# Winograd products that accumulate onto one another in PSUM, in the MLP of a two-layer hybrid encoder

## Chip, cores and metric

One core of a Trainium2 chip runs the whole kernel. The metric is the device time of one execution in microseconds (us). Before the change the median of three runs is 3536.11 us (3528.11 to 3537.86).

## The reference

The trunk has two layers over 1024 tokens of width 1024, in float32. Layer 0 mixes by grouped-query attention, layer 1 by a bidirectional gated DeltaNet. Each mixer is followed by the same MLP, and this MLP is what the change touches:

```python
def conv_ffn(h, w_up, conv_w, conv_b, w_down):
    u = depthwise_conv_centred(h @ w_up, conv_w, conv_b)
    a, b = jnp.split(u, 2, axis=-1)
    return (jax.nn.silu(a) * b) @ w_down
...
        h = h + conv_ffn(rmsnorm(h, norm_ffn[i]), ffn_w_up[i], ffn_conv_w[i],
                         ffn_conv_b[i], ffn_w_down[i])
```

D_FF is 2816, so `w_up` is 1024 x 5632 and `w_down` 2816 x 1024. The convolution runs over three neighbouring tokens.

## The kernel before, in words

Activations lie transposed: features on the 128 partitions, the 1024 tokens along the free axis in two halves of 512 (`HALVES`). A float32 product is made of three TensorE products: both operands are split into a high part (a rounding cast on ScalarE, L109) and a low part (a subtraction on VectorE or GpSimd, L110), and high x high, high x low and low x high are added in PSUM. `dense` (L126) issues them, 128x128 weights against 512 columns, one PSUM bank of 128x512 as target.

Both projections use Winograd's form of Strassen's scheme: the operands are cut in 2 x 2 blocks, seven block products are made of sums of blocks, and the four output blocks are sums of the products.

**Up projection** (`UpProjection.run`, L975). A loop over 22 values of `f`. Each makes seven products of 12 matmuls; in the order of the code before they are p1, p2 ("11", "21"), p5 ("t1"), p6 ("t2"), p7 ("t3"), p4 ("t4") and p3 ("22"). `operands` (L948) loads four 128x512 blocks of weights and forms four sums `s` of them, two on POOL and two on DVE. `product` (L967) splits an operand and calls `dense`. Seven additions on DVE (`add`, L981) and one ScalarE copy (L991) build `ua` and `ub` (128x1024) from the PSUM banks. Then the convolution: one ScalarE Identity (L1010) and two VectorE scalar_tensor_tensor (L1011, L1013) for each of `ua` and `ub`, a Silu (L1016), a product (L1017). `DownProjection.take` (L1035) stores the result in DRAM, and for odd `f` forms on POOL the token sums that the down projection will need (L1039).

**Down projection** (`DownProjection.run`, L1076). Seven products, "11", "21", "t1", "t2", "t3", "t4", "22", one after the other. Each has 11 rounds `p` (`NP`), and in a round four output tiles `m` of three matmuls each: 12 matmuls a round, 132 a product, into four banks. Weights come by DMA (`load`, L1071), tokens by DMA from DRAM and a split (`tokens`, L1064; `gh`, `gl`). `w5` (L1134) adds the blocks `a21` and `a22` into `s`; `w6` (L1144) subtracts `a11` from it; t3 takes a21 - a11, formed on POOL, and 22 takes a12 - s, formed on POOL (L1163). The residual comes back from DRAM through `res`, three buffers (L1101).

The banks matter here. PSUM has eight. The pool `mm` has two tiles of two banks (`big()`), the ring `sp` has four single banks (`bank()`). A product of the down projection before takes one `mm` tile and two `sp` banks:

```python
            acc = t.big()
            accs = [acc[:, HALVES[0]], acc[:, HALVES[1]], t.bank(), t.bank()][:len(ms)]
```

so two consecutive products stand in different banks.

The order on each engine is set by a scheduler that takes instructions by priority as they become ready; `ahead` raises the priority of a block. It is fixed when the kernel is built, and each engine then runs its list in that order, waiting at the head for what is not ready.

Of the kernel before, what the change touches and what calls it, by code (L numbers as in the profile page):

```python
# [9 lines left out]
F32 = mybir.dt.float32  # L10
# [3 lines left out]
ALU = mybir.AluOpType  # L14
# [4 lines left out]
P = 128  # L19
S = 1024  # L20
# [6 lines left out]
NP = NFF // 2  # L27
# [14 lines left out]
class Trunk:  # L42
# [80 lines left out]
            out += [(hi[:, i * n:(i + 1) * n], lo[:, i * n:(i + 1) * n]) for i in range(c)]  # L123
        return out

    def dense(self, acc, w, ys, halves=HALVES, first=True, last=True):  # L126

        n = len(ys)
        one = len(halves) == 1
        for k, ((hi, lo), (yh, yl)) in enumerate(zip(w, ys)):  # L130
            for t, (a, y) in enumerate(((hi, yh), (hi, yl), (lo, yh))):
                for hs in halves:
                    self.nc.tensor.matmul(acc if one else acc[:, hs], lhsT=a, rhs=y[:, hs],  # L133
                                          start=(first and k + t == 0), stop=(last and k == n - 1 and t == 2))

    def half_dense(self, acc, w, ys, i):

# [730 lines left out]


class UpProjection:  # L870
# [64 lines left out]
                put("22", k, xs, y[k + 4][1])  # L935

    def start(self, n):
        for _ in range(n):
            p1, p25, ua = self.begin()
            for k, (acc, name) in enumerate(((p1, "11"), (p25[:, HALVES[0]], "21"))):  # L940
                self.t.dense(acc, self.t.weights(self.src(len(self.started), 0, k)), self.b[name], [slice(0, H2)])
            self.nc.scalar.copy(out=ua[:, HALVES[0]], in_=p1)
            self.started.append((p25, ua))

    def begin(self):
        return self.t.bank(), self.t.big(), self.us.tile([P, S], F32, name="ua", bufs=2)

    def operands(self, f):  # L948
        nc, raw = self.nc, []
# [14 lines left out]
        return {"p1": (a11, "11"), "p2": (a12, "21"), "p5": (s[0], "t1"), "p6": (s[1], "t2"), "p7": (s[2], "t3"),  # L964
                "p4": (a22, "t4"), "p3": (s[3], "22")}

    def product(self, acc, ops, name):  # L967
        x, col = ops[name]
        hi, lo = self.t.pair(self.t.wp, "w", H2)
        self.t.split(x, hi, lo, self.nc.gpsimd if name in ("p6", "p4") else self.nc.vector)  # L970
        w = [(hi[:, k * P:(k + 1) * P], lo[:, k * P:(k + 1) * P]) for k in range(4)]
        self.t.dense(acc, w, self.b[col], [slice(0, H2)])
        return acc

    def run(self, up, down):  # L975

        t, nc = self.t, self.nc
        self.up, cw = up, self.cw

        def add(out, x, acc):  # L980
            nc.vector.tensor_tensor(out=out, in0=acc, in1=x, op=ALU.add)  # L981

        for f in range(NFF):
            early = f < len(self.started)
            with t.ahead(early):
                ops = self.operands(f)
            if early:
                p25, ua = self.started[f]
            else:
                p1, p25, ua = self.begin()  # L990
                nc.scalar.copy(out=ua[:, HALVES[0]], in_=self.product(p1, ops, "p1"))  # L991
                self.product(p25[:, HALVES[0]], ops, "p2")
            p2, p5 = (p25[:, hs] for hs in HALVES)
            ub = up.tile([P, S], F32, name="ub", bufs=2)
            u2 = self.us.tile([P, H2], F32, name="u2", bufs=1)
            (ua0, ua1), (ub0, ub1) = ([u[:, hs] for hs in HALVES] for u in (ua, ub))
            with t.ahead(early):
                self.product(p5, ops, "p5")
                p6 = self.product(t.bank(), ops, "p6")
            add(u2, ua0, p6)  # L1000
            add(ua0, ua0, p2)
            add(ua1, u2, p5)
            add(ub1, u2, self.product(t.bank(), ops, "p7"))
            add(ub0, ub1, self.product(t.bank(), ops, "p4"))
            add(ub1, ub1, p5)
            add(ua1, ua1, self.product(t.bank(), ops, "p3"))
            ts = []
            for u, i, n in ((ua, f, 2), (ub, NFF + f, 1)):
# [12 lines left out]


class DownProjection:
# [52 lines left out]
    def run(self):  # L1076
# [9 lines left out]
            t.split(x, *pair)  # L1086
            return pair

        def product(name, x, ms=range(4), ys=None):

            acc = t.big()
            accs = [acc[:, HALVES[0]], acc[:, HALVES[1]], t.bank(), t.bank()][:len(ms)]
            for p in range(NP):
                w = x(p)
                y = ys(p) if ys else self.tokens(name, p)
                for acc, m in zip(accs, ms):
                    t.dense(acc, [[a[:, m * P:(m + 1) * P] for a in w]], [y], [slice(0, H2)],
                            first=p == 0, last=p == NP - 1)
            return list(zip(ms, accs))

        def residual(m, i):  # L1101
            r = gm.tile([P, H2], F32, name="res", bufs=3)
# [16 lines left out]
            return weights(self.load(x, 0, 0, p), pairs[p - 3] if p > 2 else None)  # L1119

        a11 = []
        acc = product("11", w1, ys=lambda p: self.ready[p] if p < G_FIRST else self.tokens("11", p))
        base = [x[:, hs] for x in [t.base(i, F32) for i in range(8)] for hs in HALVES]
        u, a12 = base[:4], base[4:4 + NP]
        for m, acc in acc:
            nc.scalar.copy(out=u[m], in_=acc)
            add(h(m, 0), acc, residual(m, 0))
        w2 = lambda p: weights(self.load(a12[p], 0, 1, p), [one(n, p, F32R) for n in ("a21", "a22")])
        for m, acc in product("21", w2):
            add(h(m, 0), acc, h(m, 0))  # L1130
            done(m, 0, m == 0)
        a21, a22, s = (slot(n) for n in ("a21", "a22", "s"))

        def w5(p):  # L1134
            for j, a in enumerate((a21, a22)):
                self.load(a[p], 1, j, p)
            add(s[p], a21[p], a22[p])
            return weights(s[p])

        for m, acc in product("t1", w5):  # L1140
            for k in (m, 4 + m):
                add(h(k, 1), acc, residual(k, 1))

        def w6(p):  # L1144
            if p < A_LATE:
# [1 line left out]
            sub(s[p], s[p], a11[p])  # L1147
            return weights(s[p])

        for m, acc in product("t2", w6):  # L1150
            add(u[m], acc, u[m])
            add(h(m, 1), h(m, 1), u[m], nc.gpsimd)
        for m, acc in product("t3", lambda p: weights(sub(a21[p], a11[p], a21[p], nc.gpsimd))):
            add(u[m], acc, u[m])
            add(h(4 + m, 1), h(4 + m, 1), u[m], nc.gpsimd)
            done(4 + m, 1, m == 0)
            r = residual(4 + m, 0)
            add(h(4 + m, 0), r, u[m], nc.gpsimd)
        for m, acc in product("t4", lambda p: weights(a22[p])):
            add(h(4 + m, 0), acc, h(4 + m, 0))  # L1160
            done(4 + m, 0, False)
        for p in range(NP):
            sub(a12[p], a12[p], s[p], nc.gpsimd)  # L1163
        sides = [list(zip(*(slot(n, F32R) for n in names))) for names in (("a21", "a11"), ("a22", "s"))]
        for p in range(NP):
            weights(a12[p], sides[0][p])
            self.tokens("22", p, sides[1][p])
        for ms in ((0, 1, 2), (3,)):
            for m, acc in product("22", lambda p: sides[0][p], ms, lambda p: sides[1][p]):
                add(h(m, 1), acc, h(m, 1))  # L1170
                done(m, 1, False)

# [200 lines left out]
```

## Time and profile before

| | |
|---|---|
| median of 3 runs | 3536.11 us (3528.11 to 3537.86) |
| the profiled execution, its own time | 3534.62 us |
| its span, first to last instruction | 3532.7 us |
| mean granted TensorE clock | 0.98 |
| busy share PE / DVE / ACT / POOL | 94 / 75 / 47 / 31 % |
| up projection, layer 0 / layer 1 | about 670 to 1099 / 2850 to 3297 us |
| down projection, layer 0 / layer 1 | about 1099 to 1350 / 3297 to 3518 us |

Read it from the engine that is nearly always busy. PE is busy for 94% of the span, so time can be gained or lost where PE stands idle or runs at the lower clock. Everything that the other engines do beside a busy PE costs nothing. A wait is printed behind an instruction as [idle before <-releaser]. In the trace's names `mm` and `sp` are PSUM tiles, `wh`/`wl` and `gh`/`gl` split weights and tokens; in the down projection `a`, `s` and `base` are blocks of weights.

### The profile page before, as it was taken

How to read it: one execution, taken by the hardware profiler on the slowest of the kernel's cores; microseconds unless marked ns; L12 is line 12 of the kernel's file. 1: busy time of each engine (PE TensorE's matmuls, PEld its weight loads, DVE VectorE, ACT ScalarE, POOL GpSimd, SP SyncE). 2: the span in 40 equal slices, each digit the busy share in tenths (PEclk: the TensorE clock that was granted, in tenths of full speed). 3: DMA queues.
4: the chain of work that ended last, by engine and by line, in shares of the span. 5: the costliest groups of instructions: out<-in, count | busy, mean ns of one | idle time of the engine just before them, and what ended most of it. 6: DMA issues, size and time to landing. Idle time of an engine off the chain costs nothing. (4 is left out here: it accounts for less than half of the span.)

```text
span 3532.7 us, 54926 instructions
## 1 busy us (share of the span) xinstructions
PE 3309.3 (94%) x20042; PEld 2655.5 (75%) x20042; DVE 2631.9 (75%) x4273; ACT 1648.1 (47%) x2918; POOL 1097.3 (31%) x1190
## 2 busy tenths in 40 slices
PE   7999999899999898999999999999898989999988
PEld 6877878677878686777777777777676867777776
DVE  5325886899997876767767777776763889999685
ACT  4224664433434353555555455555542544434442
POOL 1111230445452423132223333222320254454141
PEclk9999999999999999999999999999999999999999
DMA  3331016323324641333242433324355723232733
GB/s 123 103 103 63 31 34 203 105 99 112 103 102 161 197 131 58 107 110 106 85 136 75 129 108 108 108 82 136 98 164 186 232 95 105 99 112 75 241 120 110
DMA packets 249806, 411.22 MB, mean 116 GB/s; under 512 B 25536, under 2 KB 76096, under 8 KB 249536
## 3 DMA queue, kind: packets, MB, share of 16 engines
q1 hardware_dynamic: 249536, 407.72, 36.6%
q8 instruction: 157, 2.57, 0.3%
q14 instruction: 113, 0.93, 0.1%
HBM read 294.77 MB, written 107.61 MB: 114 GB/s over the span
## 5 line engine op out<-in xcount | busy, mean ns | idle before, releaser
L133 PE MATMUL mm<-base,wh 128*128 128x512 f32 x896 | 372.4, 422 | 13.8 <-DVE r L816 7.4
L133 PE MATMUL sp<-base,wh 128*128 128x512 f32 (+1 forms) x1024 | 319.9, 378 | 4.1 <-ACT wh L109 3.7
L109 ACT CAST wh<-w_raw 128x512 fp32r<-128x512 f32 x275 | 169.7, 619 | 309.9 <-PE mm L133 210.6
L110 DVE TENSOR_TENSOR wl<-w_raw,wh 128x512 fp32r<-128x512 f32 x275 | 194.6, 710 | 149.4 <-ACT wh L109 138.1
L133 PE MATMUL mm<-yl,wh 128*128 128x512 f32 x736 | 287.0, 419 | 1.6 <-DVE yl L110 0.8
L133 PE MATMUL mm<-yh,wh 128*128 128x512 f32 x736 | 285.9, 417 | 2.6 <-ACT yh L109 1.5
L133 PE MATMUL mm<-yh,wl 128*128 128x512 f32 x736 | 282.3, 412 | 1.0 <-DVE wl L110 1.0
L697 POOL TENSOR_SCALAR kd<-c,yds 128x128 f32<-128x128 f32 x224 | 95.8, 438 | 556.8 <-PE cp L726 426.3
L133 PE MATMUL sp<-base,wl 128*128 128x512 f32 (+1 forms) x608 | 226.4, 373 | 16.9 <-POOL wl L110 14.0
L133 PEld LDWEIGHTS sp<-base,wh 128*128 128x128 f32 x1024 | 193.5, 189 | 40.6 <-ACT wh L109 4.4
L151 POOL TENSOR_TENSOR rs<-rs,power 128x8 f32<-128x8 f32 (+3 forms) x30 | 61.4, 2047 | 492.9 <-DVE rs L150 492.9
L133 PEld LDWEIGHTS mm<-base,wh 128*128 128x128 f32 x896 | 171.8, 192 | 43.7 <-issue 12.0
L109 ACT CAST wh<-s 128x512 fp32r<-128x512 f32 x216 | 132.5, 614 | 150.8 <-PE mm L133 57.0
L133 PE MATMUL mm<-base,wl 128*128 128x512 f32 x448 | 189.5, 423 | 0.0
L109 ACT CAST wh<-a 128x512 fp32r<-128x512 f32 x164 | 101.0, 616 | 177.7 <-PE sp L133 171.7
L444 DVE SCALAR_TENSOR_TENSOR t<-mm,gdn_cw,t 128x1023 f32<-128x1023 f32 (+1 forms) x128 | 163.0, 1276 | 7.9 <-ACT t L441 6.7
L133 PEld LDWEIGHTS mm<-yl,wh 128*128 128x128 f32 x736 | 140.6, 191 | 29.1 <-DVE yl L110 2.9
L963 POOL TENSOR_TENSOR s<-a,a 128x512 f32<-128x512 f32 x80 | 117.2, 1464 | 141.7 <-DVE s L963 57.2
L133 PEld LDWEIGHTS mm<-yh,wl 128*128 128x128 f32 x736 | 141.0, 192 | 25.9 <-DVE wl L110 1.7
L109 ACT CAST gh<-raw 128x512 fp32r<-128x512 f32 x132 | 81.8, 620 | 167.7 <-DMA raw<-g_t 118.8
L133 PEld LDWEIGHTS mm<-yh,wh 128*128 128x128 f32 x736 | 140.4, 192 | 25.9 <-ACT yh L109 2.0
L110 DVE TENSOR_TENSOR wl<-s,wh 128x512 fp32r<-128x512 f32 x174 | 156.9, 903 | 2.7 <-ACT wh L109 2.7
(556 smaller groups left out, 9799.9 us busy)
## 6 DMA issues: line engine op xcount, KB each, us to landing
a<-in_ffn_up_dram SPq DMA_DIRECT2D x160, 256.0 KB, 3.1
c<-pk SPq DMA_DIRECT2D x128, 320.0 KB, 3.0
w_raw<-in_gdn_in_dram SPq DMA_DIRECT2D x100, 256.0 KB, 3.0
g_t<-t SPq DMA_DIRECT2D x88, 256.0 KB, 2.0
raw<-g_t SPq DMA_DIRECT2D x88, 256.0 KB, 2.7
w_raw<-in_gdn_out_dram SPq DMA_DIRECT2D x68, 256.0 KB, 3.7
g<-t SPq DMA_DIRECT2D x66, 256.0 KB, 2.0
raw<-g SPq DMA_DIRECT2D x66, 256.0 KB, 3.0
```

Source lines behind the costliest of these rows:

```text
L109: self.nc.scalar.copy(out=hi, in_=src)
L110: (engine or self.nc.vector).tensor_tensor(out=lo, in0=src, in1=hi.bitcast(F32), op=ALU.subtract)
L133: self.nc.tensor.matmul(acc if one else acc[:, hs], lhsT=a, rhs=y[:, hs], start=(first and k + t == 0), stop=(last and k == n - 1 and t == 2))
L151: nc.gpsimd.tensor_tensor(out=r, in0=v, in1=self.power[:, :w], op=ALU.pow)
L444: nc.vector.scalar_tensor_tensor(out=o, in0=a, scalar=c[:, i:i + 1], in1=o, op0=ALU.mult, op1=ALU.add)
L697: nc.gpsimd.tensor_scalar(out=kd[:, e], in0=kn, scalar1=col(self.yds, e), scalar2=1.0, op0=ALU.mult, op1=ALU.mult)
L963: e.tensor_tensor(out=s[i], in0=x, in1=z, op=op)
```

## The change

Products that enter the same output sums are accumulated in the same PSUM bank: `dense` gets `onto=True`, with which its first matmul doesn't clear the bank. In the up projection p1, p6, p7, p4 go one after the other into bank `a`, p2 into `c`, p5 and p3 into `b`; between two of them the running sum is copied or added out of the bank. The order is now p1, p2, p6, p5, p7, p3, p4. There are three DVE additions and four ScalarE copies per `f` (seven and one before). In the down projection 11, t2, t3, t4 go into the four `mm` banks and t1, 22 into four `sp` banks; 21 stands in the same four `sp` banks ahead of t1. The additions of `u` are gone, 28 additions on DVE stand where 32 were, POOL's twelve additions per layer are gone, the four copies too, and the 22 subtractions a21 - a11 and a12 - s move from POOL to DVE. The number of matmuls is the same.

```diff
-    def dense(self, acc, w, ys, halves=HALVES, first=True, last=True):
+    def dense(self, acc, w, ys, halves=HALVES, first=True, last=True, onto=False):
...
-                                          start=(first and k + t == 0), stop=(last and k == n - 1 and t == 2))
+                                          start=(first and not onto and k + t == 0), stop=(last and k == n - 1 and t == 2),
+                                          skip_group_check=onto)
...
+    def first_sum(self, banks, u):
+        u = u[:, HALVES[0]]
+        self.nc.scalar.copy(out=u, in_=banks[0])
+        self.nc.vector.tensor_tensor(out=u, in0=banks[1], in1=u, op=ALU.add)
...
             with t.ahead(early):
-                self.product(p5, ops, "p5")
-                p6 = self.product(t.bank(), ops, "p6")
-            add(u2, ua0, p6)
-            add(ua0, ua0, p2)
-            add(ua1, u2, p5)
-            add(ub1, u2, self.product(t.bank(), ops, "p7"))
-            add(ub0, ub1, self.product(t.bank(), ops, "p4"))
-            add(ub1, ub1, p5)
-            add(ua1, ua1, self.product(t.bank(), ops, "p3"))
+                self.product(a, ops, "p6", onto=True)
+                nc.scalar.copy(out=ua1, in_=a)
+                self.product(b, ops, "p5")
+                nc.scalar.copy(out=ub1, in_=b)
+            self.product(a, ops, "p7", onto=True)
+            add(ub1, a)
+            self.product(b, ops, "p3", onto=True)
+            add(ua1, b)
+            self.product(a, ops, "p4", onto=True)
+            nc.scalar.copy(out=ub0, in_=a)
...
-        acc = product("11", w1, ys=lambda p: self.ready[p] if p < G_FIRST else self.tokens("11", p))
-        base = [x[:, hs] for x in [t.base(i, F32) for i in range(8)] for hs in HALVES]
-        u, a12 = base[:4], base[4:4 + NP]
-        for m, acc in acc:
-            nc.scalar.copy(out=u[m], in_=acc)
+        a = [x[:, hs] for x in (t.big(), t.big()) for hs in HALVES]
+        b = [t.bank() for _ in range(4)]
+        for m, acc in product("11", w1, a, ys=lambda p: self.ready[p] if p < G_FIRST else self.tokens("11", p)):
             add(h(m, 0), acc, residual(m, 0))
+        a12 = [x[:, hs] for x in [t.base(i, F32) for i in range(2, 8)] for hs in HALVES][:NP]
...
-        for m, acc in product("21", w2):
+        for m, acc in product("21", w2, b):
...
-        for m, acc in product("t1", w5):
-            for k in (m, 4 + m):
-                add(h(k, 1), acc, residual(k, 1))
+        b = [t.bank() for _ in range(4)]
+        for m, acc in product("t1", w5, b):
+            add(h(4 + m, 1), acc, residual(4 + m, 1))
...
-        for m, acc in product("t2", w6):
-            add(u[m], acc, u[m])
-            add(h(m, 1), h(m, 1), u[m], nc.gpsimd)
-        for m, acc in product("t3", lambda p: weights(sub(a21[p], a11[p], a21[p], nc.gpsimd))):
-            add(u[m], acc, u[m])
-            add(h(4 + m, 1), h(4 + m, 1), u[m], nc.gpsimd)
+        for m, acc in product("t2", w6, a, onto=True):
+            add(h(m, 1), acc, residual(m, 1))
+        for m, acc in product("t3", lambda p: weights(sub(a21[p], a11[p], a21[p])), a, onto=True):
+            add(h(4 + m, 1), acc, h(4 + m, 1))
             done(4 + m, 1, m == 0)
-            r = residual(4 + m, 0)
-            add(h(4 + m, 0), r, u[m], nc.gpsimd)
-        for m, acc in product("t4", lambda p: weights(a22[p])):
-            add(h(4 + m, 0), acc, h(4 + m, 0))
+
+        def w4(p):
+            pair = weights(a22[p])
+            sub(a12[p], a12[p], s[p])
+            return pair
+
+        for m, acc in product("t4", w4, a, onto=True):
+            add(h(4 + m, 0), acc, residual(4 + m, 0))
             done(4 + m, 0, False)
-        for p in range(NP):
-            sub(a12[p], a12[p], s[p], nc.gpsimd)
...
-            for m, acc in product("22", lambda p: sides[0][p], ms, lambda p: sides[1][p]):
+            for m, acc in product("22", lambda p: sides[0][p], b, ms, lambda p: sides[1][p], onto=True):
```

What this moves is seen in the engines' lists. First TensorE in layer 0's down projection, where 21 ends (last row with `a_10`) and t1 begins (rows with `wh`). Before:

```order
4214 L133 MATMUL sp<-gh,a_10_10127 128x512
4215 L133 MATMUL mm<-gh,wh 128x512 [waits Activation_49]
4216 L133 MATMUL mm<-gl,wh 128x512 [waits DVE_49]
4217 L133 MATMUL mm<-gh,wl 128x512
4218 L133 MATMUL mm<-gh,wh 128x512
```

and now:

```order
4206 L134 MATMUL sp<-gh,a_10_9989 128x512
4207 L134 MATMUL sp<-gh,wh 128x512 [waits DVE_49,Activation_49]
4208 L134 MATMUL sp<-gl,wh 128x512
4209 L134 MATMUL sp<-gh,wl 128x512
4210 L134 MATMUL sp<-gh,wh 128x512 [waits DVE_49]
4211 L134 MATMUL sp<-gl,wh 128x512
4212 L134 MATMUL sp<-gh,wl 128x512
4213 L134 MATMUL sp<-gh,wh 128x512 [waits DVE_49]
```

t1's first matmul went from a free `mm` tile into the `sp` banks that 21 has just filled; the first matmul of each `m` there waits for DVE.

Next, what DVE has in its list at that time: the sums of 21 (`h<-...,h`), behind the addition that makes t1's weights of round 7 (`s<-a_7,a_7`). Before:

```order
1111 L110 TENSOR_TENSOR gl<-raw,gh 128x512 [waits DMAHW7_49,Activation_49]
1112 L1107 TENSOR_TENSOR s_10191<-a_7_10169,a_7_10180 128x512 [waits DMAHW1_49,DMAHW0_49]
1113 L1107 TENSOR_TENSOR h_9627<-mm,h_9627 128x512 [waits PE_49]
1114 L1107 TENSOR_TENSOR h_9628<-mm,h_9628 128x512
1115 L1107 TENSOR_TENSOR h_9629<-sp,h_9629 128x512 [waits PE_49]
```

and now:

```order
1025 L1121 TENSOR_TENSOR s_10053<-a_7_10031,a_7_10042 128x512 [waits DMAHW7_49,DMAHW1_49]
1026 L1124 TENSOR_TENSOR a_7_10031<-a_7_9651,a_7_10031 128x512 [waits DVE_49]
1027 L1121 TENSOR_TENSOR h_9495<-sp,h_9495 128x512 [waits PE_49]
1028 L1121 TENSOR_TENSOR h_9496<-sp,h_9496 128x512 [waits PE_49]
1029 L1121 TENSOR_TENSOR h_9497<-sp,h_9497 128x512 [waits PE_49]
1030 L1121 TENSOR_TENSOR h_9498<-sp,h_9498 128x512 [waits PE_49]
```

The sums keep their place behind that addition, with one of the subtractions that came from POOL between them.

Last, ScalarE in the steady part of the up projection, one `f` of the list now (`ua<-sp`, `ub<-mm` and `ub<-sp` are copies out of PSUM):

```order
457 L109 CAST wh<-s 128x512 [waits PE_49,Pool_49]
458 L1021 COPY ub<-sp 128x512 [waits PE_49]
459 L1025 ACTIVATE t_6812<-ub,ffn_cw 128x1024 [waits Activation_49]
460 L1031 ACTIVATE t_6808<-t_6808 128x1024 [waits DVE_49]
461 L958 COPY ua<-sp 128x512 [waits PE_49]
462 L109 CAST wh<-s 128x512
463 L109 CAST wh<-s 128x512 [waits PE_49]
464 L109 CAST wh<-s 128x512 [waits DVE_49,PE_49,Pool_49]
465 L1013 COPY ua<-sp 128x512 [waits PE_49]
466 L109 CAST wh<-a_6825 128x512 [waits DMAHW5_49,PE_49,Activation_49]
467 L1015 COPY ub<-mm 128x512 [waits DVE_49,PE_49]
```

The copy of p1's bank (row 461), which p6 on the same bank has to wait for, stands right behind the Silu of the `f` before (row 460); before the change p6 went into another bank of the ring.

## Rows read from the trace of the kernel before

**Rows 1.** Busy time by stretch: window, length, then PE, PEld, DVE, ACT, POOL, clock, DMA.

```profile
900.00:1000.00 100.00, 99.24 (x428) 79.75 (x427) 94.27 (x98) 40.32 (x56) 49.82 (x31) 1.00 0.30 102
1100.00:1200.00 100.00, 87.33 (x359) 69.34 (x358) 77.51 (x91) 41.54 (x70) 30.09 (x19) 0.95 0.72 240
```

**Rows 2.** Timeline, PE, layer 0's down: start us, us, instruction, [idle before <-releaser].

```profile
1158.08 0.39 PE L133 MATMUL mm<-gh,a 128*128 128x512 f32 x1
...
1160.80 0.39 PE L133 MATMUL mm<-gh,wh 128*128 128x512 f32 x1
...
1171.96 0.50 PE L133 MATMUL mm<-gh,wh 128*128 128x512 f32 x1 [2.85 <-ACT wh L109]
...
1174.87 0.80 PE L133 MATMUL mm<-gh,wl 128*128 128x512 f32 x1 [2.17 <-DVE wl L110]
...
1175.89 0.63 PE L133 MATMUL mm<-gl,wh 128*128 128x512 f32 x1
1176.32 0.63 PE L133 MATMUL mm<-gh,wl 128*128 128x512 f32 x1
...
1285.75 0.50 PE L133 MATMUL mm<-gh,wl 128*128 128x512 f32 x1 [2.01 <-DVE wl L110]
...
1308.80 0.39 PE L133 MATMUL mm<-a,a 128*128 128x512 f32 x1
```

**Rows 3.** Timeline, PE, layer 1's down: first matmul of t1, first of 22.

```profile
3338.55 0.39 PE L133 MATMUL mm<-gh,wh 128*128 128x512 f32 x1
...
3484.65 0.39 PE L133 MATMUL mm<-a,a 128*128 128x512 f32 x1
```

**Rows 4.** Timeline, DVE, layer 0's down, from the end of 21 into t2.

```profile
1166.63 0.69 DVE L1107 TENSOR_TENSOR s<-a,a 128x512 f32<-128x512 f32 x1
1167.24 1.28 DVE L1107 TENSOR_TENSOR h<-mm,h 128x512 f32<-128x512 f32 x2
...
1191.48 1.75 DVE L110 TENSOR_TENSOR wl<-s,wh 128x512 fp32r<-128x512 f32 x1
...
1209.51 0.68 DVE L110 TENSOR_TENSOR wl<-s,wh 128x512 fp32r<-128x512 f32 x1
```

**Rows 5.** Timeline, POOL, the same stretch.

```profile
1190.97 3.40 POOL L1110 TENSOR_TENSOR base<-base,s 128x512 f32<-128x512 f32 x2
```

**Rows 6.** Busy time of 10 us in t1, layer 0.

```profile
1170.00:1180.00 10.00, 5.86 (x14) 4.37 (x15) 9.85 (x13) 5.08 (x10) 3.88 (x3) 0.71 0.96 333
```

**Rows 7.** Timeline, DVE, layer 1's down, at the end of 21.

```profile
3343.61 0.69 DVE L1107 TENSOR_TENSOR s<-a,a 128x512 f32<-128x512 f32 x1 [2.05 <-DMA a<-in_ffn_down_dram]
...
3349.05 0.68 DVE L1107 TENSOR_TENSOR s<-a,a 128x512 f32<-128x512 f32 x1
```

**Rows 8.** DMA issues from 1130 to 1240 us: KB each, median us to landing.

```profile
res<-xf SPq DMA_DIRECT2D x12, 256.0 KB, 4.1
```

**Rows 9.** Waits of PE: 720 to 1099 us, then 2890 to 3297 (total us, times, longest).

```profile
PE sp L133 <- POOL wl L110: 5.4, 7, 1.3
...
PE sp L133 <- POOL wl L110: 8.1, 10, 2.5
```

**Rows 10.** Groups by line, DVE and ACT, 720 to 1099 us: busy us, mean ns, idle.

```profile
L1013 DVE SCALAR_TENSOR_TENSOR t<-ub,ffn_cw,t 128x1023 f32<-128x1023 f32 x19 | 44.0, 2316 | 0.0
L1011 DVE SCALAR_TENSOR_TENSOR t<-ua,ffn_cw,t 128x1023 f32<-128x1023 f32 x19 | 24.3, 1279 | 0.0
L981 DVE TENSOR_TENSOR ub<-sp,ub 128x512 f32<-128x512 f32 x20 | 13.7, 685 | 9.2 <-PE sp L133 9.2
...
L1010 ACT ACTIVATE t<-ua,ffn_cw 128x1024 f32<-128x1024 f32 x19 | 23.6, 1241 | 0.0
L1016 ACT ACTIVATE t<-t 128x1024 f32<-128x1024 f32 x19 | 20.2, 1062 | 36.3 <-DVE t L1013 36.3
L991 ACT COPY ua<-sp 128x512 f32<-128x512 f32 x19 | 11.0, 577 | 0.0
```

**Rows 11.** Timeline, PE, layer 0, early in the up projection.

```profile
701.21 0.50 PE L133 MATMUL sp<-110h,wl 128*128 128x512 f32 x1 [2.36 <-DVE wl L110]
```

More of the change, by code (lines that the diff above doesn't have):

```diff
@@ L938, in start, with halves @@
         for _ in range(n):
[L939 to L943, printed above, removed]
-    def begin(self):
-        return self.t.bank(), self.t.big(), self.us.tile([P, S], F32, name="ua", bufs=2)
+            f, banks, u = len(self.started), *self.begin()
+            for k, (acc, name) in enumerate(zip(banks, ("11", "21"))):
+                self.t.dense(acc, self.t.weights(self.src(f, 0, k)), self.b[name], [slice(0, H2)])
+            self.first_sum(banks, u)
+            self.started.append((banks, u))
+    def begin(self):
+        c, b = (x for x in self.halves(self.t.big()))
+        return (self.t.bank(), c, b), self.us.tile([P, S], F32, name="ua", bufs=2)
+    @staticmethod
+    def halves(x):
+        return [x[:, hs] for hs in HALVES]
+    def first_sum(self, banks, u):
+        u = u[:, HALVES[0]]
+        self.nc.scalar.copy(out=u, in_=banks[0])
+        self.nc.vector.tensor_tensor(out=u, in0=banks[1], in1=u, op=ALU.add)
     def operands(self, f):
@@ L965, in operands, with product @@
                 "p4": (a22, "t4"), "p3": (s[3], "22")}
-    def product(self, acc, ops, name):
+    def product(self, acc, ops, name, onto=False):
         x, col = ops[name]
@@ L971, in product @@
         w = [(hi[:, k * P:(k + 1) * P], lo[:, k * P:(k + 1) * P]) for k in range(4)]
-        self.t.dense(acc, w, self.b[col], [slice(0, H2)])
-        return acc
+        self.t.dense(acc, w, self.b[col], [slice(0, H2)], onto=onto)
     def run(self, up, down):
@@ L978, in run, with add @@
         self.up, cw = up, self.cw
-        def add(out, x, acc):
-            nc.vector.tensor_tensor(out=out, in0=acc, in1=x, op=ALU.add)
+        def add(u, acc):
+            nc.vector.tensor_tensor(out=u, in0=acc, in1=u, op=ALU.add)
         for f in range(NFF):
@@ L987, in run @@
             if early:
-                p25, ua = self.started[f]
+                banks, ua = self.started[f]
             else:
[L990 to L993, printed above, removed]
+                banks, ua = self.begin()
+                self.product(banks[0], ops, "p1")
+                self.product(banks[1], ops, "p2")
+                self.first_sum(banks, ua)
+            a, _, b = banks
             ub = up.tile([P, S], F32, name="ub", bufs=2)
-            u2 = self.us.tile([P, H2], F32, name="u2", bufs=1)
-            (ua0, ua1), (ub0, ub1) = ([u[:, hs] for hs in HALVES] for u in (ua, ub))
+            (_, ua1), (ub0, ub1) = (self.halves(u) for u in (ua, ub))
             with t.ahead(early):
-                self.product(p5, ops, "p5")
-                p6 = self.product(t.bank(), ops, "p6")
-            add(u2, ua0, p6)
-            add(ua0, ua0, p2)
-            add(ua1, u2, p5)
-            add(ub1, u2, self.product(t.bank(), ops, "p7"))
-            add(ub0, ub1, self.product(t.bank(), ops, "p4"))
-            add(ub1, ub1, p5)
-            add(ua1, ua1, self.product(t.bank(), ops, "p3"))
+                self.product(a, ops, "p6", onto=True)
[8 more added lines that the diff above has]
+            nc.scalar.copy(out=ub0, in_=a)
             ts = []
@@ L1087, in weights, with product @@
             return pair
-        def product(name, x, ms=range(4), ys=None):
-            acc = t.big()
-            accs = [acc[:, HALVES[0]], acc[:, HALVES[1]], t.bank(), t.bank()][:len(ms)]
+        def product(name, x, accs, ms=range(4), ys=None, onto=False):
             for p in range(NP):
@@ L1095, in product @@
                 y = ys(p) if ys else self.tokens(name, p)
[L1096 to L1099, printed above, removed]
+                for m in ms:
+                    t.dense(accs[m], [[a[:, m * P:(m + 1) * P] for a in w]], [y], [slice(0, H2)],
+                            first=p == 0, last=p == NP - 1, onto=onto)
+            return [(m, accs[m]) for m in ms]
         def residual(m, i):
@@ L1134, in w5 @@
         def w5(p):
-            for j, a in enumerate((a21, a22)):
-                self.load(a[p], 1, j, p)
+            for j, x in enumerate((a21, a22)):
+                self.load(x[p], 1, j, p)
             add(s[p], a21[p], a22[p])
             return weights(s[p])
-        for m, acc in product("t1", w5):
-            for k in (m, 4 + m):
-                add(h(k, 1), acc, residual(k, 1))
+        b = [t.bank() for _ in range(4)]
+        for m, acc in product("t1", w5, b):
+            add(h(4 + m, 1), acc, residual(4 + m, 1))
         def w6(p):
```

## The prediction

> **What bounds the kernel now.** I read the busy time by stretch first. In the steady up projection PE is busy for 99.24 of 100 us at full clock, though DVE is at 94.27 [rows 1]. DVE work saved there is worth nothing unless PE waits for it, and PE waits for little: 5.4 us in layer 0 and 8.1 us in layer 1, each time for the weights that POOL splits [rows 9]. In the down projection it is otherwise: 87.33 of 100 us, the clock at 0.95 [rows 1]. So the place to look at is the down projection, and there I read PE's timeline.
>
> A round of 12 matmuls takes 1160.80 - 1158.08 = 2.72 us at full clock [rows 2], a product of 11 rounds 29.9 us. From the first matmul of t1 (1160.80) to the first of 22 (1308.80) there are four products, 119.7 us of work, and 148.0 us passed: **28.3 us lost**. In layer 1 it is 3484.65 - 3338.55 = 146.1 us [rows 3], **26.4 us lost**. Some of this is waiting, mostly for DVE's `wl` (2.17 and 2.01 us and six others) and once for ACT's `wh` (2.85) [rows 2]; the rest is the half clock that follows a wait (0.71 granted in one window of 10 us [rows 6]).
>
> Why is DVE late there? A `wl` of 128x512 takes 1.75 us at 1191.48 and 0.68 us at 1209.51 [rows 4]. In the first case POOL is at its subtractions a12 - s and a21 - a11, 3.40 us for two, back to back [rows 5]. The same DVE instruction is 2.6 times as long while POOL reads and writes SBUF beside it.
>
> **Down projection, what goes.** The 22 subtractions leave POOL for DVE, and with the twelve additions POOL has nothing left in this stage. A DVE operation then costs about 0.61 us (from 1166.63 to 1167.24 [rows 4]) in place of about 1.7. The order of the changed kernel has 37 DVE rows after 21's sums up to the weights of t1's last round, four of the moved subtractions included: 37 x 0.61 = 22.6 us, while PE needs 10 rounds, 27.2 us, before that. DVE is no longer late, and I take the lost 28.3 and 26.4 us as gone, t4's wait of 2.01 us among them, 54.7 us together.
>
> **Down projection, what comes.** Three new waits stand against it.
>
> (1) t1 now goes into the `sp` banks that 21 has filled, so PE waits until DVE has added 21 to h. These additions stand in DVE's list behind the addition for round 7, which ran at 1166.63 because its weights came late, and now behind one moved subtraction too. They so begin at 1166.63 + 2 x 0.61 = 1167.85 and the first ends near 1168.5: PE is idle for 1168.5 - 1160.8 = 7.7 us. The three others follow 0.6 us apart, and PE needs 0.68 us per tile, so they cost nothing more. In layer 1 the addition for round 8 stands ahead too; round 7's ran at 3343.61 after a wait for its DMA and round 8's at 3349.05 [rows 7]. With its weights landed in time the sums begin about 1.8 us after 3343.61 and the first ends at 3346.1, 7.5 us after 3338.55; at the latest they end after 3349.05, 11.5 us. I take 8. Below, both could shrink to nothing if the loads came early.
>
> (2) The clock. After the pair of waits 2.85 and 2.17 one matmul follows another after 0.43 us (1175.89 to 1176.32 [rows 2]) where full clock gives 2.72 / 12 = 0.23. In the window that holds this the clock is 0.71 [rows 6]: 29% of 10 us is about 3 us. I take 3 us per layer, and 0 to 5 as bounds.
>
> (3) t3 goes onto t2's banks. Its first matmul on tile m needs the sum of t2's tile m, which became complete 2.04 us (three tiles) earlier; the addition takes 0.7 us. For m = 0 to 2 nothing waits. The fourth needs a fourth `res` tile, whose DMA can go out only when the first addition has freed one of three buffers; 4.1 us to landing [rows 8]. It is ready at 0.7 + 4.1 + 0.7 = 5.5 us, PE is there at 2.04 + 3 x 0.68 = 4.1: 1.4 us, bounds 0 and 3. t4 onto t3 has no such load and costs nothing.
>
> Per layer 7.7 + 3 + 1.4 = 12.1 us and 8 + 3 + 1.4 = 12.4 us. **Down projection: -54.7 + 24.5 = -30 us**, bounds -50 and -10.
>
> One rule speaks against this edit: the Trainium skill, Perfetto Trace Analysis, section Matmuls, wants independent groups of matmuls to rotate through banks so that the reading of one overlaps the next group. The row at 1160.80, where t1 begins without a gap, agrees with it. By that rule each of the reused banks costs its reading, and the sum would be the first rival's below.
>
> **Up projection.** Per f four DVE additions (0.685 us each [rows 10]) go, three ACT copies of 0.577 us come. ACT and DVE lie beside PE. What can be gained is the 13.5 us of [rows 9]; POOL's `wl` is no part of the edit, DVE's shorter list only lets POOL's inputs come earlier, so I take -1. The new wait: p6 goes onto p1's bank after ACT's copy, which stands behind the Silu. From the end T of the f before: ua's last addition ends near T - 2.0 (p3 now comes before p4), the Identity (1.24) at T - 0.7, the two convolution steps (1.28 and at worst 2.32) at T + 2.9 to 3.3, the Silu (1.06) at T + 4.0 to 4.4, the copy at T + 4.6 to 5.0 [rows 10]. p6 starts after p1 and p2, 2.72 us each, at T + 5.4. About half a microsecond of room: no wait, but not much room. The other reuses (p7, p3, p4) have a whole product of 2.7 us between. Bounds: -13 and, if the room is missed by 0.5 us in 40 of the f, +20.
>
> An early f waits for DVE's `wl` (2.36 us [rows 11]) while DVE has a backlog; four additions less are 2.7 us. I take -3, bounds -8 and +8. At the end of the down projection the norm of the next stage finds free `mm` tiles before 22 ends: -1.5, bounds -6 and 0.
>
> **Sum.** -30 - 1 - 3 - 1.5 = -35.5 us against the profiled execution of 3534.6 us, which is 1.5 us below the median: **3499 us**. About 0.3% (10.6 us) is what a measurement of this kernel can tell from no change.
>
> **Rivals.**
> - *The banks aren't free in time in the up projection: slower.* If the chain Silu, copy, p6 is late by more than half a microsecond, every f pays. The point that decides is 35 us over 40 steady f, 0.9 us per f: DVE delays of a second 1.75 us subtraction ahead of the convolution steps would do it. At 1.2 us per f the time is 3499 + 48 = 3547 us. If each of the four reuses cost its copy of 0.577 us, 2.3 us per f, it is 3591. For it: DVE at 94% and POOL at 50 of 100 us. Against it: 0.5 us of room, 2.2 on the others, and DVE is relieved by 2.7 us per f. The rule of the Trainium skill cited above gives this end. Chance 0.11.
> - *DVE stays the bound in t1 and t2: about the same.* Late DMAs stop DVE's list (2.05 us once [rows 7]; the loads ran at 333 GB/s, 0.96 of the engines' time, in that window [rows 6]), and with 22 more subtractions on it half of the 54.7 us stays: -35.5 + 27 = -8 us, 3526 us. Chance 0.15.
> - *The waits are smaller and up gains too: faster still.* Loads land earlier, (1) falls to 3 us per layer and POOL's waits go: -55 us, 3480 us. Chance 0.09.
> - The forecast, -17 to -50 us: chance 0.65.
>
> **Range and chances.** The low end 3474 takes in the third rival and the lower bounds of the down projection and the first f together (-50 - 8 - 3); the high end 3536 takes in the second and no more than the start of the first. Left out are most of the first rival (0.10) and some 0.08 below. Faster by over 0.3%: forecast 0.65, third 0.09, under half of the second 0.06, in all 0.80. Within 0.3%: 0.10. Slower: 0.10.
>
> **What would show it.** In the changed profile PE's row at the start of t1 should have an idle of 7 to 9 us ahead of it, ended by DVE's sum `h<-sp,h`; DVE's `wl` in t1 and t2 should take 0.68 us; POOL should be empty in the down projection; from t1's first matmul to 22's there should be about 124 us (119.7 + 3 + 1.4) instead of 148. In the steady up projection PE should be at 99 of 100 us as now. I am wrong if PE there waits for `ua<-sp` or for weights by more than 0.9 us per f, or if t1's rounds still wait for `wl`.

## The result, and the profile after

The changed kernel takes 3502.26 us (median of 4 runs, 3501.20 to 3503.66), the kernel before 3536.99 us beside it (4 runs, 3528.11 to 3539.30): a ratio of 0.9901, 95% interval 0.9889 to 0.9912, or 35 us less. The forecast was 3499 us, 35.5 us below the profiled execution of before. The profiled execution of the changed kernel took 3503.66 us, its span is 3501.9 us.

The stage that was to change, layer 0's down projection, in the busy time by stretch (columns as in [rows 1]; PE first, POOL fifth):

```profile
900.00:1000.00 100.00, 99.63 (x425) 78.82 (x424) 76.34 (x77) 49.74 (x73) 46.75 (x31) 1.00 0.31 106
1100.00:1200.00 100.00, 92.60 (x397) 75.48 (x396) 75.76 (x116) 41.40 (x69) 4.91 (x3) 0.97 0.79 260
```

POOL's 30.09 us [rows 1] became 4.91, PE's 87.33 became 92.60; from 21's end to 22 POOL does nothing. In the steady up projection DVE fell from 94 to 76 of 100 us and PE stayed where it was.

PE's timeline shows the boundaries of the stage. In layer 0 the rows are the last matmul of 21, the first of t1, the first wait in t3, and the first of 22; then the last of 21, the first of t1 and the first of 22 in layer 1:

```profile
1155.50 0.39 PE L134 MATMUL sp<-gh,a 128*128 128x512 f32 x1
1163.12 0.77 PE L134 MATMUL sp<-gh,wh 128*128 128x512 f32 x1 [7.23 <-DVE h L1121]
...
1225.72 0.47 PE L134 MATMUL mm<-gh,wh 128*128 128x512 f32 x1 [0.39 <-DVE h L1121]
...
1286.33 0.39 PE L134 MATMUL sp<-a,a 128*128 128x512 f32 x1
...
3321.95 0.39 PE L134 MATMUL sp<-gh,a 128*128 128x512 f32 x1
...
3330.54 0.77 PE L134 MATMUL sp<-gh,wh 128*128 128x512 f32 x1 [8.21 <-DVE h L1121]
...
3453.80 0.39 PE L134 MATMUL sp<-a,a 128*128 128x512 f32 x1
```

21 ends one step of 0.23 us after its last matmul's start. From there to 22 it is 1286.33 - 1155.73 = 130.6 us in place of 148.0 [rows 2], and 3453.80 - 3322.18 = 131.6 us in place of 146.1 [rows 3]. Every wait for `wl` in between is gone; what stands there now is the wait for 21's sums, 7.23 and 8.21 us. PE's waits in layer 0's t1 to t4 (total us, times, longest), before

```profile
PE mm L133 <- DVE wl L110: 14.8, 8, 4.1
PE mm L133 <- ACT wh L109: 2.8, 1, 2.8
```

and after, with DVE's timeline ahead of the sums of 21, and the busy time of the 10 us behind them (clock third from the end):

```profile
PE sp L134 <- DVE h L1121: 7.2, 1, 7.2
PE mm L134 <- ACT ssq L174: 0.4, 1, 0.4
PE mm L134 <- DVE h L1121: 0.4, 1, 0.4
...
1160.95 0.69 DVE L1121 TENSOR_TENSOR s<-a,a 128x512 f32<-128x512 f32 x1 [1.87 <-DMA a<-in_ffn_down_dram]
1161.67 0.69 DVE L1124 TENSOR_TENSOR a<-a,a 128x512 f32<-128x512 f32 x1
1162.28 2.48 DVE L1121 TENSOR_TENSOR h<-sp,h 128x512 f32<-128x512 f32 x4
...
1163.00:1173.00 10.00, 9.88 (x34) 8.02 (x35) 8.96 (x15) 5.36 (x9) 0.00 (x0) 0.77 0.86 284
```

The sums of 21 begin at 1162.28, behind the addition that waited for its DMA and one moved subtraction.

Against the end of the span, stretch by stretch (starts of matmuls, us):

| stretch | before | after | difference |
|---|---|---|---|
| to the down projection of layer 0 | 1099.2 | 1095.1 | -4.1 |
| its products 11 and 21 | 61.6 | 60.6 | -1.0 |
| from 21's end to 22 | 148.0 | 130.6 | -17.4 |
| 22, to the next layer's first matmul | 33.9 | 33.9 | 0.0 |
| DeltaNet mixer, to the MLP's norm | 1450.1 | 1456.9 | +6.8 |
| that norm, up projection, 11 and 21 | 545.8 | 545.0 | -0.8 |
| from 21's end to 22 | 146.1 | 131.6 | -14.5 |
| 22 and the final norm, to the end | 48.1 | 48.1 | 0.0 |

The fifth row is not the change's: each engine's list of instructions for the mixer is the same in both kernels, only line and buffer numbers differ. Its length differs from execution to execution: in the profile of the changed kernel run once more (below) it is 2774.25 - 1324.58 = 1449.7 us. The two profiled executions lie 31 us apart with these 6.8 us in them, the medians 35. Of the first row's 4.1 us, 3.0 lie ahead of the up projection's first product. The rows of the mixer's two ends, before

```profile
1342.68 0.70 PE L133 MATMUL mm<-base,wh 128*128 128x512 f32 x2 [0.94 <-ACT base L109]
...
2792.77 0.38 PE L157 MATMUL mm<-ones,ssq 128*128 128x1 f32 x2 [0.32 <-DVE ssq L176]
```

and after:

```profile
1320.25 0.62 PE L134 MATMUL mm<-base,wh 128*128 128x512 f32 x2
...
2777.16 0.61 PE L159 MATMUL mm<-ones,ssq 128*128 128x1 f32 x4 [0.32 <-DVE ssq L178]
```

Last, DVE's splits of t1's and t2's weights, grouped by line from 1155 to 1260 us (busy us, mean ns), before

```profile
L110 DVE TENSOR_TENSOR wl<-s,wh 128x512 fp32r<-128x512 f32 x20 | 20.1, 1006 | 0.7 <-ACT wh L109 0.7
```

and after, with the two groups of subtractions that came from POOL:

```profile
L110 DVE TENSOR_TENSOR wl<-s,wh 128x512 fp32r<-128x512 f32 x19 | 13.0, 685 | 2.6 <-ACT wh L109 2.5
...
L1124 DVE TENSOR_TENSOR a<-a,a 128x512 f32<-128x512 f32 x11 | 7.3, 682 | 0.0
L1124 DVE TENSOR_TENSOR base<-base,s 128x512 f32<-128x512 f32 x11 | 7.1, 684 | 0.0
```

The mean fell from 1006 to 685 ns. The 22 moved operations cost DVE 14.4 us.

### The profile page after: what moved, and what is told of

It is laid out like the page before. It is cut to its first block, busy times and chain, and to the rows that moved or that the text cites. A ratio compares the mean times of both kernels' runs of the same rounds, so it can differ in the third digit from the quotient of the medians.

```text
span 3501.9 us, 54777 instructions
## 1 busy us (share of the span) xinstructions
PE 3305.3 (94%) x20042; PEld 2651.2 (76%) x20042; DVE 2449.4 (70%) x4133; ACT 1722.5 (49%) x3042; POOL 959.9 (27%) x1122
## 5 line engine op out<-in xcount | busy, mean ns | idle before, releaser
L134 PE MATMUL mm<-base,wh 128*128 128x512 f32 x1248 | 480.3, 412 | 12.5 <-DVE r L818 7.4
L134 PEld LDWEIGHTS mm<-base,wh 128*128 128x128 f32 x1248 | 237.5, 190 | 55.9 <-issue 11.9
L134 PE MATMUL mm<-base,wl 128*128 128x512 f32 x624 | 257.3, 412 | 0.0
L109 ACT CAST wh<-s 128x512 fp32r<-128x512 f32 x216 | 134.1, 621 | 222.1 <-PE sp L134 108.8
L134 PE MATMUL sp<-base,wh 128*128 128x512 f32 (+1 forms) x672 | 210.1, 370 | 1.5 <-DVE ub L995 0.9
L110 DVE TENSOR_TENSOR wl<-s,wh 128x512 fp32r<-128x512 f32 x174 | 144.9, 834 | 23.4 <-ACT wh L109 23.0
L134 PE MATMUL sp<-base,wl 128*128 128x512 f32 (+1 forms) x432 | 157.2, 364 | 1.6 <-DVE wl L110 1.6
L976 POOL TENSOR_TENSOR s<-a,a 128x512 f32<-128x512 f32 x80 | 105.8, 1323 | 158.4 <-DVE s L976 99.6
L134 PEld LDWEIGHTS sp<-base,wh 128*128 128x128 f32 x672 | 126.4, 188 | 24.2 <-ACT wh L109 2.0
L1054 POOL TENSOR_TENSOR t<-t,t 128x512 f32<-128x512 f32 x66 | 102.6, 1555 | 126.4 <-DVE t L1032 124.5
```

The lines of the kernel that those rows point to most:

```text
L109: self.nc.scalar.copy(out=hi, in_=src)
L110: (engine or self.nc.vector).tensor_tensor(out=lo, in0=src, in1=hi.bitcast(F32), op=ALU.subtract)
L976: e.tensor_tensor(out=s[i], in0=x, in1=z, op=op)
L1054: sub = lambda out, x, z: nc.gpsimd.tensor_tensor(out=out, in0=x, in1=z, op=ALU.subtract)
```

## The experiments

The theory: the gain is in the down projection, and there it is POOL's leaving SBUF to DVE. The rivals: the gain is the sums that PSUM makes for nothing, or it is the up projection.

**One projection at a time.** The first kernel has the changed `DownProjection` and the old `UpProjection`, the second the other way round.

> The changed down projection with the up projection as it was before. Theory (the gain lies in the down projection, about 17 us in layer 0 and 15 us in layer 1 between the end of 21 and the first matmul of 22): 3505 us, 32 us below before. Rival (the up projection gives a third or more of it): 3515 us or more.

Measured: 3500.39 us, ratio 0.9915 (0.9896 to 0.9934).

> The changed up projection with the down projection as it was before. Theory: 3532 us, 5 us below before, since PE is bound there and only the waits for POOL's weights (13 us in both layers) could go. Rival: 3520 us or less. In the trace an f takes 19.81 us on the mean of two where it took 19.90 before.

Measured: 3530.60 us, ratio 1.0002 (0.9990 to 1.0014). The down projection alone gives 30 of the 35 us, and the intervals allow all of them. The up projection gives nothing that can be measured, where 5 us had been expected.

**The subtractions alone, both ways.** The changed kernel with the 22 subtractions back on POOL:

```diff
-        for m, acc in product("t3", lambda p: weights(sub(a21[p], a11[p], a21[p])), a, onto=True):
+        for m, acc in product("t3", lambda p: weights(sub(a21[p], a11[p], a21[p], nc.gpsimd)), a, onto=True):
...
-            sub(a12[p], a12[p], s[p])
+            sub(a12[p], a12[p], s[p], nc.gpsimd)
             return pair
```

> The changed kernel with the 22 subtractions per layer (a21 - a11 and a12 - s) back on POOL. Theory (DVE's operations are stretched while POOL works on SBUF, and that made PE wait in t1 and t2): wl takes 1.7 us again there, the 130.6 us from the end of 21 to the first matmul of 22 become 150 to 158, the time 3540 to 3555 us. Rival (the gain comes from the sums that PSUM makes, fewer additions on DVE and POOL): 3502 to 3512 us, or less, since DVE has 22 operations fewer per layer.

Measured: 3523.85 us, ratio 0.9980 (0.9969 to 0.9992), beside 0.9901 of the change. From 21's end to 22 it is 145.5 us in layer 0 and 145.9 in layer 1, 15 and 14 us more than in the changed kernel. DVE's timeline in t1 and t2, and PE's waits there:

```profile
1182.87 3.44 DVE L1124 TENSOR_TENSOR s<-s,a 128x512 f32<-128x512 f32 x2
1186.23 1.76 DVE L110 TENSOR_TENSOR wl<-s,wh 128x512 fp32r<-128x512 f32 x1
```

```profile
1158.57 0.76 PE L134 MATMUL sp<-gh,wh 128*128 128x512 f32 x1 [7.65 <-DVE h L1121]
...
1181.32 0.80 PE L134 MATMUL sp<-gh,wl 128*128 128x512 f32 x1 [3.73 <-DVE wl L110]
...
1188.05 0.50 PE L134 MATMUL sp<-gh,wl 128*128 128x512 f32 x1 [1.26 <-DVE wl L110]
```

A `wl` takes 1.76 us again and PE waits for it, although this kernel has 22 DVE operations fewer per layer than the changed one. What is left of the gain, 7 us with an interval that lies below 1, is what the rest of the change gives with the subtractions on POOL; in the stage itself it is 2.7 us in this profile (145.5 and 145.9 against 148.0 and 146.1). The time is below the 3540 to 3555 us that the theory gave: that figure was reckoned from 3502 and 150 to 158 us in the stage, and the stage took 145.5.

The opposite: the kernel before, with nothing but the 22 subtractions moved to DVE (both `nc.gpsimd` left out), banks and additions as they were.

> The kernel before with only the 22 subtractions per layer moved from POOL to DVE; no product accumulates onto another, banks as before. Theory: the waits for wl go and no wait for a bank comes, 148 us become 122 to 128 in layer 0, the time 3485 to 3495 us, less than the changed kernel's 3502. Rival (fewer additions are the gain): DVE has 22 operations more per layer, 3537 us or more.

Measured: 3503.30 us, ratio 0.9925 (0.9907 to 0.9942). This alone is about 26 of the 35 us, so the rival of the fewer additions falls as the main cause. But the time is 8 us above the theory's range: from 21's end to 22 it is 131.1 and 134.1 us, not 122 to 128. Two of PE's seven waits in layer 0:

```profile
1168.06 0.50 PE L133 MATMUL mm<-gh,wl 128*128 128x512 f32 x1 [1.03 <-DVE wl L110]
...
1174.72 0.50 PE L133 MATMUL mm<-gh,wl 128*128 128x512 f32 x1 [0.94 <-DVE wl L110]
```

No wait for a bank, but waits of 0.75 to 1.03 us for `wl` and t4's of 2.01 us, as before. `wl` itself takes 0.68 us here. That DVE's list, with 32 additions a layer on the sums and 22 subtractions, is a little too long is the likely reason; it was not tried. Accumulating takes these waits away and pays with the wait at 21's banks: in the stage the two come out nearly even, 131.1 + 134.1 = 265.2 us without it and 130.6 + 131.6 = 262.2 us with it.

**The changed kernel once more**, as a measure for what follows.

> The changed kernel once more, as the measure for the three beside it. Both theories: 0.990 of the time of before, as measured already.

Measured: 3497.58 us beside 3531.84, ratio 0.9903 (0.9889 to 0.9916).

**What eats the up projection's gain.** In the changed kernel PE no longer waits for POOL's weights ([rows 9] before), yet f still takes 19.8 us on the mean of two. Product p1 starts in the steady part at these times, eight pairs of f apart, before

```profile
741.88 0.40 PE L133 MATMUL sp<-110h,wh 128*128 128x512 f32 x1
...
1060.21 0.40 PE L133 MATMUL sp<-110h,wh 128*128 128x512 f32 x1
```

and after:

```profile
738.58 0.40 PE L134 MATMUL sp<-110h,wh 128*128 128x512 f32 x1
...
758.55 0.40 PE L134 MATMUL sp<-110h,wh 128*128 128x512 f32 x1
...
1055.48 0.40 PE L134 MATMUL sp<-110h,wh 128*128 128x512 f32 x1
```

That is 318.33 / 16 = 19.90 us and 316.90 / 16 = 19.81 us. The mean hides a trade: every second f, the short one, took 19.41 us before and takes 19.63 now; the long ones between took 19.5 to 21.0 and take 19.98 (from 780 us on, layer 0). PE's list gives a lead. In 42 of the 44 f p5's first matmul waits for DVE, which it did not before in any (PE's list of the changed kernel):

```
2437 L134 MATMUL mm<-t10h,wh 128x512 [waits DVE_49,Activation_49]
```

On the chip one such wait is printed in full, early in layer 0, and the later ones are a step of 0.52 us where 0.23 is usual:

```profile
706.19 0.47 PE L134 MATMUL mm<-t10h,wh 128*128 128x512 f32 x1 [2.71 <-DVE ua L959]
...
944.82 0.40 PE L134 MATMUL sp<-t23h,wl 128*128 128x512 f32 x1
945.34 0.48 PE L134 MATMUL mm<-t10h,wh 128*128 128x512 f32 x1
```

What DVE ends just before, at 945.19 us (`ua<-mm,ua`, 0.68 us from 944.51), is the addition of p2's bank, the other half of the PSUM tile into which p5 goes. First attempt: put that addition behind p5 in the program.

```diff
-                self.first_sum(banks, ua)
-            a, _, b = banks
+                nc.scalar.copy(out=ua[:, HALVES[0]], in_=banks[0])
+            a, c, b = banks
...
                 self.product(b, ops, "p5")
+                add(ua0, c)
                 nc.scalar.copy(out=ub1, in_=b)
```

> The changed kernel, but DVE's addition of p2's bank to ua stands behind p5 in the program. Theory (p5's first matmul waits in every f for that addition, which reads the other half of p5's PSUM tile, and this gives back what the up projection gains): the wait of 2.71 us for ua goes in both layers, an f takes 19.5 to 19.7 us on the mean of two instead of 19.81, the time is 8 to 15 us below the changed kernel. Rival (the weights set p5's start, the addition only ends beside it): within 3 us of the changed kernel.

Measured: 3522.09 us, ratio 0.9967 (0.9955 to 0.9980), 25 us above the changed kernel. Half of the theory is seen: p5's wait is gone, and the short f takes 19.42 us (p1 starts at 721.81 and 741.23 us). But every second f takes 21.3 us, which neither the theory nor its rival had, and the trace says why. ACT's timeline, then DVE's, then PE's at p3:

```profile
919.27 0.59 ACT L1016 COPY ub<-mm 128x512 f32<-128x512 f32 x1 [3.25 <-DVE ua L995]
```

```profile
916.27 1.76 DVE L976 TENSOR_TENSOR s<-s,a 128x512 f32<-128x512 f32 x1 [2.44 <-POOL s L976]
917.95 0.68 DVE L110 TENSOR_TENSOR wl<-s,wh 128x512 fp32r<-128x512 f32 x1
918.55 0.68 DVE L995 TENSOR_TENSOR ua<-mm,ua 128x512 f32<-128x512 f32 x1
```

```profile
919.90 0.74 PE L134 MATMUL mm<-base,wh 128*128 128x512 f32 x2 [1.60 <-ACT ub L1016]
```

ACT's copy of p5's half waits for DVE's addition of p2's half, which stands behind an operation that waits for POOL; and p3, which goes onto p5's bank, waits for the copy. This is what the first rival of the prediction speaks of, a bank that isn't free in time, but at p3 and not at p6: a wait of 1.60 us, and 1.3 us more than the 19.98 us of the changed kernel, in every second f.

So this order is no remedy; the shared tile ties the three engines together in either order. Second attempt: p2 gets a bank of its own from the ring, the order is the changed kernel's.

```diff
-        c, b = (x for x in self.halves(self.t.big()))
-        return (self.t.bank(), c, b), self.us.tile([P, S], F32, name="ua", bufs=2)
+        b = self.t.big()[:, HALVES[1]]
+        return (self.t.bank(), self.t.bank(), b), self.us.tile([P, S], F32, name="ua", bufs=2)
```

> The changed kernel, but p2 goes into a bank of the ring of single banks instead of the other half of the tile of p5 and p3; the order of the program is the changed kernel's. Theory (accesses to the two halves of one PSUM tile are put in a row, so p5 waits for DVE's addition of p2, and in the kernel before this the copy of p5 waited for it): p5's wait for ua goes, the short f takes 19.4 us instead of 19.63, none takes more than 20, the time is 5 to 14 us below the changed kernel. Rival (the lists of ACT and DVE are too full for the copies, as in the kernel with the addition later): an f of 21 us again, 10 us or more above the changed kernel.

Measured: 3488.48 us beside 3534.41, ratio 0.9874 (0.9859 to 0.9890). p5's matmul has no wait for DVE in its list any more, and in the steady part no wait of PE is printed at all. Starts of p1, as above:

```profile
736.38 0.40 PE L134 MATMUL sp<-110h,wh 128*128 128x512 f32 x1
...
756.37 0.40 PE L134 MATMUL sp<-110h,wh 128*128 128x512 f32 x1
...
1051.59 0.40 PE L134 MATMUL sp<-110h,wh 128*128 128x512 f32 x1
```

315.21 / 16 = 19.70 us per f, the short f 19.4 and the long one 20.0. In the steady part the gain is the short f's 0.22 us; the long one is as in the changed kernel. This version beats the kernel before by some 45 us, and the changed one by about 10: its interval lies below that of the change (0.9889 to 0.9912) but for 0.0001.

**The wait for 21's banks.** DVE's list ahead of 21's sums held operations that wait for DMAs. Moved to POOL: t1's additions from round 5 and t3's subtractions from round 7.

```diff
-            add(s[p], a21[p], a22[p])
+            add(s[p], a21[p], a22[p], nc.gpsimd if p > 4 else nc.vector)
...
-        for m, acc in product("t3", lambda p: weights(sub(a21[p], a11[p], a21[p])), a, onto=True):
+        for m, acc in product("t3", lambda p: weights(sub(a21[p], a11[p], a21[p], nc.vector if p < A_LATE else nc.gpsimd)), a, onto=True):
```

> The changed kernel, but t1's additions of rounds 5 to 10 and t3's subtractions of rounds 7 to 10 are on POOL, so that no operation that waits for a DMA of a21 or a22 stands ahead of 21's sums in DVE's list. Theory (the wait of 7.2 and 8.2 us at the start of t1 is DVE's list held up by DMAs, not the additions' own time): the wait falls to 1 to 4 us, and the time by 5 to 12 us. Rival (PE waits for the additions themselves, or the twelve POOL operations cost DVE as much): 3 us less or no less.

Measured: 3499.03 us, ratio 0.9908 (0.9895 to 0.9922), no change, as the rival had it; the wait is 6.82 and 7.42 us. DVE's timeline shows that another operation took the place of the one moved:

```profile
1158.22 1.77 DVE L110 TENSOR_TENSOR gl<-raw,gh 128x512 fp32r<-128x512 f32 x1 [1.99 <-ACT gh L109]
1159.91 2.47 DVE L1121 TENSOR_TENSOR h<-sp,h 128x512 f32<-128x512 f32 x4
```

It is a split of tokens for t1, which waits for ScalarE's cast of them, and that cast waits 2.07 us for its DMA. With this kernel alone the theory stayed open. So these splits went to POOL too, for t1's rounds 3 to 7 (`tokens` passes an engine on to `split`):

```diff
-                y = ys(p) if ys else self.tokens(name, p)
+                y = ys(p) if ys else self.tokens(name, p, None, nc.gpsimd if name == "t1" and 2 < p < 8 else None)
```

> The kernel with the sums earlier, with the low parts of t1's tokens of rounds 3 to 7 on POOL too, so that ahead of 21's sums DVE's list has only what 21 and the first three rounds of t1 need. Theory (the wait at the start of t1 is DVE's list held up by DMAs; in the kernel with the sums earlier it was held by tokens instead of weights): the wait falls from 6.8 to 1 to 4 us, the time by 4 to 10 us, less what POOL's work costs DVE. Rival (the wait is the additions' own): 6.5 to 7.5 us again.

Measured: 3511.98 us, ratio 0.9935 (0.9922 to 0.9948). PE in layer 0:

```profile
1160.16 0.47 PE L134 MATMUL sp<-gh,wh 128*128 128x512 f32 x1 [1.91 <-DVE h L1121]
1170.41 0.50 PE L134 MATMUL sp<-gh,wl 128*128 128x512 f32 x1 [1.35 <-DVE wl L110]
1178.44 0.50 PE L134 MATMUL sp<-gl,wh 128*128 128x512 f32 x1 [2.40 <-POOL gl L110]
1181.86 0.80 PE L134 MATMUL sp<-gh,wl 128*128 128x512 f32 x1 [2.92 <-DVE wl L110]
```

The wait fell to 1.91 us (5.55 in layer 1), so in layer 0 it was the list and not the additions; in layer 1 that is shown only in part. But with POOL at work in t1 PE waits for `wl` again, and for POOL itself, and the stage takes 135.8 us instead of 130.6; the kernel is some 11 us slower than the changed one. Moving this work to POOL does not pay for the wait.

Combinations. The sums earlier together with the later addition of p2:

> The edits of the two kernels before this one together. Theory: their gains add up, 13 to 25 us below the changed kernel, 3478 to 3490 us where the changed kernel takes 3500. Rival: one of them or neither counts, less than 10 us.

Measured: 3522.44 us, ratio 0.9973 (0.9963 to 0.9983): neither helps. The bank of its own together with the freed list:

> The edits of the two kernels before this one together. If both theories hold, 9 to 22 us below the changed kernel; if one falls, the other's alone.

Measured: 3500.37 us, ratio 0.9908 (0.9895 to 0.9922): what the one gains the other loses. In its profile the wait in layer 0 is 5.63 us again, though the same operations are on POOL: DVE stands 4.77 us at the split of tokens that is last ahead of the sums. Again it is the list, and the edit frees it only at times.

**Is accumulating worth anything in the down projection?** The up projection with p2 in its own bank, and the down projection of before with the subtractions moved.

> The up projection of the kernel with p2 in a bank of its own, and the down projection of the kernel before with only the 22 subtractions moved to DVE (no product accumulates onto another there). Theory (in the down projection the gain is the subtractions' move, and accumulating gives with fewer additions what it takes with the wait for 21's banks): 0.985 to 0.990 of before, within 6 us of the 0.9874 of the kernel with p2 in its own bank. Rival (accumulating is worth a third or more of the gain): 0.991 or more.

Measured: 3489.52 us, ratio 0.9881 (0.9864 to 0.9897). It can't be told from the 0.9874 of the same up projection with the changed down projection. So with the subtractions on DVE the gain in the down projection is that move, and accumulating adds nothing that these runs can tell from zero.

## Why the prediction was right, point by point

- **What goes in the down projection.** Right in place and cause. DVE's `wl` takes 0.685 us there, PE waits for none, and putting the subtractions back costs 15 and 14 us. Of the time from 21's end to 22, 130.6 and 131.6 us, 119.7 are work: 10.9 and 11.9 us lost, where 12.1 and 12.4 were forecast. The Trainium skill (SBUF — State Buffer, Who interferes with whom) says that a `tensor_tensor` with both inputs in SBUF contends with GpSimd's reads; 1.76 us with POOL at work and 0.68 without agree with it.
- **(1), the wait for 21's banks.** 7.7 and 8 us forecast, 7.23 and 8.21 measured. The additions stood behind a late DMA and one moved subtraction, as read from the list.
- **(2), the clock, and (3), t3's wait.** From t1's first matmul to 22's it is 1286.33 - 1163.12 = 123.2 us, of which 119.7 are work; 124.1 were forecast. Behind the wait the first matmuls of t1 follow one another after 0.43 us where full clock gives 0.23, until 1167.8; that is 2.2 us, and the clock granted in the 10 us from 1163 is 0.77. t3 waited 0.39 us instead of 1.4, and at its first tile, not at its fourth; t4, forecast at nothing, waited as long; with the slower steps at its start each lost 0.6 us. In PE's list the first matmul of either waits for DVE's sum of tile 1, which lies in the other half of the PSUM tile, and not of tile 0 alone.
- **Sum of the down projection.** -17.4 - 14.5 = -31.9 us measured in the profiled execution, -30 forecast, and -30 us in the runs of the kernel with this part alone (0.9915 of 3530.57).
- **Up projection.** The step that failed is "The other reuses (p7, p3, p4) have a whole product of 2.7 us between": it overlooked p5, which waits for DVE's addition of p2 out of the other half of its tile. The waits for POOL's weights did go, but 0.1 us per f is all that was left of it: from the seventh p1 on, the two layers together gained 1.7 us where -1 was forecast. The term that came out wrong is the early f's -3. From the first p1 to the seventh it is 137.3 us in layer 0 (138.1 before) and 138.5 in layer 1 (136.9 before), +0.8 us together, and the printed wait of 2.71 us for p2's addition lies there; with p2 in its own bank layer 1 takes 136.9 again. The runs of this part alone show 0 with an interval of about 4 us either way, where -4 was forecast. The room of half a microsecond for p6 held.
- **End of the down projection.** -1.5 us forecast for the norm, 0.0 measured in both layers; why nothing came of it was not looked into.
- **The total.** 35.5 us forecast and 35 measured in the medians is closer than the parts are: the runs of the two parts alone give 30 and 0 us, and the forecast's other 5.5 us did not come as such. That the sum hit so well is in part luck; a few us between medians are within the intervals.
- **The rivals.** The first was closer than its 0.11 says: one addition moved in the program made a bank late at p3, at 25 us. The rule cited in the prediction (the Trainium skill, Perfetto Trace Analysis, section Matmuls) is borne out in that a bank taken up at once makes PE wait: 7.23 and 8.21 us at t1, where DVE's list was held up, and 0.39 us each at t3 and t4, which go onto the banks just filled as well. DVE as the bound in t1 and t2 did not come.

## What to carry to other kernels

Ask first which engine is late and what stretches its instructions; here moving 22 subtractions per layer off GpSimd was worth about 26 of the 35 us of a much larger rewrite, and beside the mended up projection it could not be told from the rewritten down projection. An accumulation chain in one bank ties TensorE to the reader of that bank, so read from the readers' lists what stands ahead of each reading, and look at what shares the reader's PSUM tile as well as its bank. Where a small part of a forecast fails, print the step between two products in the steady loop: waits of 0.1 to 0.3 us were not among the printed waits here, but the loop's period had them.

## What the runs showed that I had not expected

- Two halves of one PSUM tile are tied in this kernel. In the changed kernel p5's matmul, and in the kernel with the later addition ACT's copy of p5's half, waited for DVE's reading of the other half. With p2 in a tile of its own both waits were gone and 9 us with them (3497.58 and 3488.48 us, ratios 0.9903 and 0.9874). The waits stand in the engines' lists, where they come from how the kernel is built; whether the chip itself would need them was not tried.
- The DeltaNet mixer took 6.8 us longer in the one profiled execution than in the other with the same lists on all engines, and 7.2 us longer than in another execution of the very same kernel. A difference of a few us between two profiled executions says nothing by itself; the stretch has to be one that the change touches.
